# Softmax over 32768 columns: each block of eight partitions takes every sixteenth 64 KB half row, in place of one half row per partition in order

## The chip, the cores and the metric

The kernel runs on one core of one Trainium2 chip. The metric is the device time of one execution in microseconds (us), lower is better. Verdicts use the fast runs alone, with a 95% interval. Ratios are the mean time of one kernel's fast runs over that of the kernel before in the same rounds, so they are not quite the ratios of the medians quoted beside them.

## The reference, cut to what matters

```python
batch, seq, vocab = 16, 256, 32768          # float32, temperature 1.0
scaled = logits / temperature
scaled = scaled - scaled.max(axis=-1, keepdims=True)
exp_scaled = np.exp(scaled)
return exp_scaled / exp_scaled.sum(axis=-1, keepdims=True)
```

There are 4096 rows of 128 KB. All of the input (536.87 MB) has to come in, and as much has to go out.

## The kernel before

A row is cut into two halves of 64 KB, and 128 half rows make a group, one on each partition. A group is loaded in two chunks of 128 x 8192 elements (4 MB, 32 KB on each partition). Six chunk buffers keep loads and stores running side by side. Maximum and sum are exchanged between the two partitions of a row with a shuffle.

```python
_SPLIT = 2
_CW = 8192
_BUFS = 6
_LAST_DMA = 4096
# ...
    x = xf.rearrange("n (h v) -> (n h) v", h=_SPLIT)
    o = of.rearrange("n (h v) -> (n h) v", h=_SPLIT)
# ...
    def load(i: int) -> None:
        g, c = divmod(i, C)
        xs = xpool.tile([P, CW], fp32, tag="x", name="xs")
        slots[i] = xs
        for s, n in spans(CW, _LAST_DMA if g in (0, G - 1) else CW):
            tc.keep_in_program_order(
                nc.sync.dma_start(
                    out=xs[:, s : s + n],
                    in_=x[g * P : (g + 1) * P, c * CW + s : c * CW + s + n],
                )
            )
# ... store(i) is the mirror image; only the last group is stored in 2 MB pieces
    def combine(v, op) -> None:
        for j in range(n_rounds):                    # one round
            mask = [i ^ (1 << j) for i in range(32)]
            nc.vector.stream_shuffle(out=v[:, j + 1 : j + 2], in_=v[:, j : j + 1], mask=mask)
# ...
    order = [("L", i) for i in range(min(_BUFS, n_chunks))] + [("S", 0)]
    for i in range(1, n_chunks):
        order.append(("S", i))
        if i + _BUFS - 1 < n_chunks:
            order.append(("L", i + _BUFS - 1))
```

So six chunks of loads are issued before any store. From then on one store and one load follow each other on one queue.

Of the kernel before, what the change touches and what calls it, by code (L numbers as in the profile page):

```python
# [6 lines left out]


_SPLIT = 2
_CW = 8192  # L10
_BUFS = 6
_PIECE = 8192
# [5 lines left out]
def kernel(  # L18
# [8 lines left out]
    P = nc.NUM_PARTITIONS  # L27
# [6 lines left out]
    xf = logits.flatten_outer_dims()  # L34
    of = out.flatten_outer_dims()
    N, V = xf.shape
    W = V // _SPLIT
    CW = min(_CW, W)
    C = W // CW
    assert W * _SPLIT == V and CW * C == W and (N * _SPLIT) % P == 0  # L40
    x = xf.rearrange("n (h v) -> (n h) v", h=_SPLIT)
    o = of.rearrange("n (h v) -> (n h) v", h=_SPLIT)
    G = N * _SPLIT // P
    n_chunks = G * C
    n_rounds = _SPLIT.bit_length() - 1
# [6 lines left out]
    def spans(total: int, step: int) -> list[tuple[int, int]]:  # L52
        return [(s, min(step, total - s)) for s in range(0, total, step)]
# [4 lines left out]
# [5 lines that stand above are left out]
            tc.keep_in_program_order(  # L63
                nc.sync.dma_start(  # L64
                    out=xs[:, s : s + n],
                    in_=x[g * P : (g + 1) * P, c * CW + s : c * CW + s + n],
                )
            )

    def store(i: int) -> None:  # L70
        g, c = divmod(i, C)
        xs = slots.pop(i)
        for s, n in spans(CW, _LAST_DMA if g == G - 1 else CW):
            tc.keep_in_program_order(
                nc.sync.dma_start(  # L75
                    out=o[g * P : (g + 1) * P, c * CW + s : c * CW + s + n],
                    in_=xs[:, s : s + n],
                )
            )

    def combine(v, op) -> None:
        for j in range(n_rounds):
            mask = [i ^ (1 << j) for i in range(32)]
            nc.vector.stream_shuffle(  # L84
                out=v[:, j + 1 : j + 2], in_=v[:, j : j + 1], mask=mask
            )
            nc.vector.tensor_tensor(  # L87
                out=v[:, j + 1 : j + 2],
                in0=v[:, j : j + 1],
                in1=v[:, j + 1 : j + 2],  # L90
                op=op,
            )
# [30 lines left out]
    def factors(g: int) -> None:  # L123
        nm, ssum, ee, f, ttj = stats[g]
        nMh = spool.tile([P, 1 + n_rounds], fp32, tag="nMh", name="nMh")
        Sh = spool.tile([P, 1 + n_rounds], fp32, tag="Sh", name="Sh")
        rS = spool.tile([P, 1], fp32, tag="rS", name="rS")
        with tc.high_priority():
            nc.vector.tensor_reduce(out=nMh[:, 0:1], in_=nm, axis=X, op=A.min)  # L129
            combine(nMh, A.min)  # L130
            nc.scalar.activation(  # L131
                out=ee,
                in_=nm,
                func=Exp,
                bias=nMh[:, n_rounds : n_rounds + 1],
                scale=-1.0,
            )
            nc.vector.tensor_tensor_reduce(  # L138
                out=ttj,
                in0=ee,  # L140
                in1=ssum,
                scale=1.0,
                scalar=0.0,
                op0=A.mult,
                op1=A.add,
                accum_out=Sh[:, 0:1],
            )
            combine(Sh, A.add)
            nc.vector.reciprocal(out=rS, in_=Sh[:, n_rounds : n_rounds + 1])  # L149
            nc.vector.tensor_scalar_mul(out=f, in0=ee, scalar1=rS)  # L150
# [28 lines left out]
    for kind, i in order:  # L179
        if kind == "L":  # L180
            load(i)
            loaded = i + 1
        else:
            g = i // C
            if g > done:
                while nxt < (g + 1) * C:
                    assert nxt < loaded
                    exps(nxt)
                    nxt += 1
                factors(g)  # L190
                done = g
            scales(i)
            store(i)
# [35 lines left out]
```

## Time and profile before

| | before |
|---|---|
| median of 4 runs | 2494.8 us (2492.84 to 2495.53) |
| DMA, share of 16 engines' span | 99.9% |
| DVE, ACT busy | 60%, 56% |
| bytes moved | 1073.74 MB |
| 32 KB packets (32000 of them) | median 1213 ns, mean 1215 ns |

The next lines are from the page of the kernel before. They are the engines' busy times; the rate of the DMA in 40 equal slices of the span; its queue (packets, MB, share of 16 engines' time); and the chain of work that ended last, as shares of the span.

```profile
DVE 1487.4 (60%) x964; ACT 1405.0 (56%) x455; POOL 0.2 (0%) x4
...
GB/s 412 433 430 432 429 431 432 433 433 434 433 434 432 435 432 435 432 435 431 436 431 435 432 434 433 434 433 433 433 433 433 433 433 434 434 433 434 432 431 368
...
q1 hardware_dynamic: 37728, 1073.76, 99.9%
...
DMA 96%; SPq 1%; ACT 1%; DVE 1%; issue 1%; ACTq 0%
```

The chain is nearly all DMA, and the rate is flat at about 433 GB/s from the second slice to the last but one. The compute engines have 40% to spare, so they do not matter here. The packet records say why the rate is flat: almost every 32 KB packet took the same 1213 ns, which is 27.0 GB/s for an engine and 432 GB/s for sixteen.

The first loads, in the timeline of the kernel before (start, duration, engine, line, operation; the reduction is the first work on loaded data):

```profile
0.73 3.92 SPq L64 DMA_DIRECT2D xs<-in_logits_dram  x8
...
12.89 8.69 DVE L107 TENSOR_REDUCE nm<-xs 128x1 f32<-128x8192 f32 x1 [12.89 <-DMA xs<-in_logits_dram]
```

What the DMA-issuing queue waited for, in us in total, times, and the longest:

```profile
SPq L64 <- DMA out_dram<-xs: 2246.9, 122, 19.6
```

### The profile page before, as it was taken

The numbers are of one execution on the slowest core, as the hardware profiler recorded it, in microseconds if no ns is written. First come the engines' busy times: TensorE is split into PE (matmuls) and PEld (weight loads), VectorE is DVE, ScalarE is ACT, GpSimd is POOL, SyncE is SP. The second block draws the span as 40 slices with busy tenths as digits, with TensorE's granted clock in tenths as the row PEclk, the third lists the DMA queues.
The fourth block names the chain that finished last, engine by engine and source line by source line (L and its number), as shares of the span: only waits on it lengthen the run. The fifth ranks groups of instructions, "written<-read, shape, count | busy, mean of one in ns | idle before, by whom it ended". The sixth has DMA issues, their size and how long they took to land.

```text
span 2493.8 us, 2234 instructions
## 1 busy us (share of the span) xinstructions
DVE 1487.4 (60%) x964; ACT 1405.0 (56%) x455; POOL 0.2 (0%) x4
## 2 busy tenths in 40 slices
DVE  7655565556655566555665566655666566655663
ACT  5665554655556555565555655555546555465553
POOL 0000000000000000000000000000000000000000
DMA  9999999999999999999999999999999999999998
GB/s 412 433 430 432 429 431 432 433 433 434 433 434 432 435 432 435 432 435 431 436 431 435 432 434 433 434 433 433 433 433 433 433 433 434 434 433 434 432 431 368
DMA packets 37745, 1073.90 MB, mean 431 GB/s; under 512 B 4192, under 2 KB 4192, under 8 KB 4192
## 3 DMA queue, kind: packets, MB, share of 16 engines
q1 hardware_dynamic: 37728, 1073.76, 99.9%
q14 instruction: 17, 0.14, 0.0%
HBM read 536.87 MB, written 536.87 MB: 431 GB/s over the span
## 4 chain that ended last, share of the span: by engine, by line
DMA 96%; SPq 1%; ACT 1%; DVE 1%; issue 1%; ACTq 0%
DMA out_dram<-xs 93%; DMA xs<-in_logits_dram 2%; SPq L64 1%; DVE nm L107 1%; ACT xs L163 1%; ACT xs L114 0%; ACTq L224 0%; SPq L75 0%; DVE f L150 0%; ACT ee L131 0%; DVE rS L149 0%; DVE Sh L87 0%; DVE ttj L138 0%; DVE Sh L84 0%; DVE Sh L138 0%
## 5 line engine op out<-in xcount | busy, mean ns | idle before, releaser
L114 ACT ACTIVATE xs<-xs,nm 128x8192 f32<-128x8192 f32 (+1 forms) x130 | 912.1, 7016 | 972.4 <-DVE nm L107 972.4
L107 DVE TENSOR_REDUCE nm<-xs 128x1 f32<-128x8192 f32 (+1 forms) x130 | 1111.6, 8551 | 527.3 <-DMA xs<-in_logits_dram 527.3
L163 ACT ACTIVATE xs<-xs,f 128x4096 f32<-128x4096 f32 (+1 forms) x130 | 468.1, 3648 | 71.4 <-DVE f L150 71.4
L160 DVE TENSOR_SCALAR xs<-xs,f 128x4096 f32<-128x4096 f32 (+1 forms) x130 | 295.7, 2318 | 3.7 <-DVE f L150 1.8
L138 DVE CUSTOM_DVE_ANT_0 ttj<-ee,ssum 128x2 f32<-128x2 f32 x64 | 10.3, 161 | 423.8 <-ACT ee L131 423.8
L114 ACT ACTIVATION_READ_ACCUMULATOR xs<-xs,nm 128x1 f32 x130 | 24.2, 186 | 0.0
L131 ACT ACTIVATE ee<-nm,nMh 128x2 f32<-128x2 f32 x64 | 17.9, 280 | 0.0
L150 DVE TENSOR_SCALAR f<-ee,rS 128x2 f32<-128x2 f32 x64 | 14.6, 229 | 2.2
L149 DVE RECIPROCAL rS<-Sh 128x1 f32<-128x1 f32 x64 | 10.5, 164 | 2.2
L87 DVE TENSOR_TENSOR nMh<-nMh 128x1 f32<-128x1 f32 x64 | 10.2, 160 | 2.2
L87 DVE TENSOR_TENSOR Sh<-Sh 128x1 f32<-128x1 f32 x64 | 10.2, 160 | 2.2
L129 DVE TENSOR_REDUCE nMh<-nm 128x1 f32<-128x2 f32 x64 | 9.9, 155 | 2.2
L84 DVE STREAM_SHUFFLE nMh<-nMh 128x1 f32<-128x1 f32 x64 | 9.7, 151 | 0.0
L84 DVE STREAM_SHUFFLE Sh<-Sh 128x1 f32<-128x1 f32 x64 | 9.7, 151 | 0.0
L114 ACT ACT_TABLE_LOAD x1 | 1.3, 1283 | 12.9 <-DMA xs<-in_logits_dram 12.9
L138 DVE DVE_READ_ACCUMULATOR2_ANT Sh<- 128x1 f32 x64 | 5.3, 84 | 0.0
L84 DVE LOAD_MASK_SELECT Sh<-Sh x64 | 0.9, 14 | 2.8
L84 DVE LOAD_MASK_SELECT nMh<-nMh x64 | 0.9, 14 | 2.7
L210 POOL MEMSET const-bfloat16-1.0<- 128x1 bf16 x1 | 0.1, 102 | 0.0
L210 POOL MEMSET const-uint8-127<- 128x1 uint8 x1 | 0.1, 102 | 0.0
L210 POOL MEMSET const-float32-0.0<- 128x1 f32 x1 | 0.1, 99 | 0.2 <-issue 0.2
L210 POOL MEMSET const-float32-1.0<- 128x1 f32 x1 | 0.1, 99 | 0.0
## 6 DMA issues: line engine op xcount, KB each, us to landing
out_dram<-xs SPq DMA_DIRECT2D x126, 4096.0 KB, 38.2
xs<-in_logits_dram SPq DMA_DIRECT2D x124, 4096.0 KB, 29.0
xs<-in_logits_dram SPq DMA_DIRECT2D x8, 2048.0 KB, 22.3
out_dram<-xs SPq DMA_DIRECT2D x4, 2048.0 KB, 26.7
```

The source lines that it names most:

```text
L64: nc.sync.dma_start(out=xs[:, s : s + n], in_=x[g * P : (g + 1) * P, c * CW + s : c * CW + s + n],)
L84: nc.vector.stream_shuffle(out=v[:, j + 1 : j + 2], in_=v[:, j : j + 1], mask=mask)
L87: nc.vector.tensor_tensor(out=v[:, j + 1 : j + 2], in0=v[:, j : j + 1], in1=v[:, j + 1 : j + 2], op=op,)
L107: nc.vector.tensor_reduce(out=nm[:, k : k + 1], in_=xs[:, s : s + n], axis=X, op=A.max, negate=True)
L114: nc.scalar.activation(out=xs[:, s : s + n], in_=xs[:, s : s + n], func=Exp, bias=nm[:, k : k + 1], scale=inv_t, accum_out=ssum[:, k : k + 1],
L129: nc.vector.tensor_reduce(out=nMh[:, 0:1], in_=nm, axis=X, op=A.min)
L131: nc.scalar.activation(out=ee, in_=nm, func=Exp, bias=nMh[:, n_rounds : n_rounds + 1], scale=-1.0,)
L138: nc.vector.tensor_tensor_reduce(out=ttj, in0=ee, in1=ssum, scale=1.0, scalar=0.0, op0=A.mult, op1=A.add, accum_out=Sh[:, 0:1],)
L149: nc.vector.reciprocal(out=rS, in_=Sh[:, n_rounds : n_rounds + 1])
L150: nc.vector.tensor_scalar_mul(out=f, in0=ee, scalar1=rS)
L160: nc.vector.tensor_scalar_mul(out=xs[:, s : s + cut], in0=xs[:, s : s + cut], scalar1=f[:, k : k + 1])
L163: nc.scalar.activation(out=xs[:, s + cut : s + n], in_=xs[:, s + cut : s + n], func=Copy, scale=f[:, k : k + 1],)
```

## The change

The intent is that DMA engines which are neighbours work on half rows which are neighbours in DRAM. Partition 8a+b now holds half row a+16b of its group, so the DRAM side of each DMA has three dimensions, 16 x 8 x columns. The two halves of a row then lie eight partitions apart.

```diff
+_OUTER = 16
+_INNER = 8
 ...
-    x = xf.rearrange("n (h v) -> (n h) v", h=_SPLIT)
-    o = of.rearrange("n (h v) -> (n h) v", h=_SPLIT)
+    x = xf.rearrange(
+        "(g b s) (h v) -> g (s h) b v", h=_SPLIT, b=_INNER, s=_OUTER // _SPLIT
+    )
+    o = of.rearrange(
+        "(g b s) (h v) -> g (s h) b v", h=_SPLIT, b=_INNER, s=_OUTER // _SPLIT
+    )
 ...
-                    in_=x[g * P : (g + 1) * P, c * CW + s : c * CW + s + n],
+                    in_=x[g, :, :, c * CW + s : c * CW + s + n],
 ...
-                    out=o[g * P : (g + 1) * P, c * CW + s : c * CW + s + n],
+                    out=o[g, :, :, c * CW + s : c * CW + s + n],
 ...
-            mask = [i ^ (1 << j) for i in range(32)]
+            mask = [i ^ (_INNER << j) for i in range(32)]
```

More of the change, by code (lines that the diff above doesn't have):

```diff
@@ L39 @@
     C = W // CW
-    assert W * _SPLIT == V and CW * C == W and (N * _SPLIT) % P == 0
-    x = xf.rearrange("n (h v) -> (n h) v", h=_SPLIT)
-    o = of.rearrange("n (h v) -> (n h) v", h=_SPLIT)
+    assert W * _SPLIT == V and CW * C == W and (N * _SPLIT) % P == 0 and _OUTER * _INNER == P
+    x = xf.rearrange(
[4 more added lines that the diff above has]
+    )
     G = N * _SPLIT // P
```

## The prediction

> What bounds the kernel now. The DMA. The page gives DMA busy 99.9% of 16 engines' span, 431 GB/s over 2493.8 us and 432 to 436 in the middle slices; DVE is busy 60%, ACT 56%. The chain of waits is 93% landings of the store, each about 38.25 us for one 4 MiB store and one 4 MiB load, back to back. The trace's packets are 32 KB half-row pieces, nearly all of exactly 1213 ns: 27.0 GB/s for each engine, 432 GB/s for 16. [...]better HBM locality can save only the ramp and the tail: 1073.74 MB at 432 GB/s is 2485 us by this estimate, so at most about 0.5% is to be had.
>
> What the change does. Compute is untouched: same instruction counts, same shapes, same 32 KB packets; the two STREAM_SHUFFLEs of a group cost 151 ns each[...]. DMA issues, now with a three-dimensional DRAM side, may cost more than the 0.49 us each read from the first eight; with 262 issues and an otherwise waiting SP queue that is off the chain.
>
> What it may break is which engine moves which partitions. [...]each should fall to half rate, 2426 ns a packet[...]. In the trace the lags between engines, read from the 16 landings of each DMA, are about 0.4 us at the start and then stay for hundreds of us (eight engines within 0.5 us, the others up to 10 us late at the end), so nothing in the kernel forces pairs apart or together. Full lockstep would make the kernel 2 x 2485 = 4970 us[...]. [...]
>
> Weighing: conflict-free or self-sorting pairs, within 2%, 0.36; conflict through part or all of the run, 0.62; a real gain over 2% contradicts the packet rate, 0.02. Predicted 2850 us, 8 in 10 between 2485 and 4600.
>
> What would show each step. Packets: [...]durations spread between 1213 and about 2430 ns and GB/s falls below 432 from the first loads on; the page's DMA busy share stays near 99%, because packets take longer. DVE and ACT busy times unchanged (1487 and 1405 us). SP waits grow on store landings. If it is wrong: packets stay 1213 ns and every slice about 433 GB/s.
>
> What would make this wrong. [...]HBM may dislike the new order[...], which would also lengthen packets and would need an experiment to tell apart.

The forecast came to 2850 us (2485 to 4600), a weighing between two ends that stand on the trace: about 2495 us if no engine slows another (the time of the kernel before), and 2 x 2485 = 4970 us if every packet took 2426 ns, twice the measured 1213 ns, to the end. That better HBM locality can save only the ramp and the tail is an estimate from the even 1213 ns alone; experiment 1, at 2495.75 us, shows no gain. "Each" is an engine in step with another that slows it; "pairs" are such engines. The shuffles took 151 ns in both kernels, with either mask.

## More of the kernel before

Windows of the kernel before (stretch, length, busy times of DVE, ACT and POOL, clock, DMA share, GB/s). Up to about 50 us there are only loads.

```profile
20.00:60.00 40.00, 38.12 (x22) 33.57 (x10) 0.00 (x0) 1.00 1.02 434
60.00:100.00 40.00, 32.50 (x25) 31.76 (x12) 0.00 (x0) 1.00 0.99 424
...
2000.00:2400.00 400.00, 241.24 (x152) 224.67 (x72) 0.00 (x0) 1.00 1.00 433
```

## The result, and the profile after

The changed kernel takes 2635.95 us in the median of 4 runs (2605.82 to 2641.83), against 2494.8 us. The ratio is 1.0541, interval 1.0473 to 1.0609: slower. Its own runs spread over 36 us, where those of the kernel before spread over 3 us. The profiled run is the fastest of them (span 2604.0 us, 110.2 us more than before).

The same lines from the page of the changed kernel:

```profile
DVE 1487.8 (57%) x964; ACT 1405.2 (54%) x455; POOL 0.2 (0%) x4
...
GB/s 210 230 283 418 406 430 434 434 430 430 433 432 431 433 434 434 433 433 432 434 433 432 433 433 434 434 433 431 433 434 434 433 431 433 434 433 432 431 387 284
...
q1 hardware_dynamic: 37728, 1073.76, 99.8%
...
DMA 91%; DVE 2%; another core or an unknown queue 2%; SPq 2%; ACT 1%; issue 0%; ACTq 0%; DVEq 0%
```

The compute is untouched and the DMA is as "busy" as before. The busy share does not show how fast the packets go: it is 1.00 at 210 GB/s (60 to 100 us) and 1.00 at 432 GB/s (2000 to 2400 us). The rate shows the loss, and it lies at the two ends. Each slice is 65.1 us. The first six slices fall short of 433 GB/s by 621 GB/s in sum, and 621/433 x 65.1 gives 93 us; the last two by 195, which gives 29 us. The same sums for the kernel before (slices of 62.3 us; 31 and 67 GB/s short) are 4 us and 10 us. The difference is 89 us at the start and about 20 us at the end, 109 of the 110 us. In between nothing is lost in this run. It is the fastest one, and no trace of the others was kept; their median is 141 us up, so some 31 us more stand in no trace of this kernel. The trace of experiment 2 (the same split, 2630.67 us) loses, by the same sum, 95 us at the start, 24 us in the middle and 30 us at the end, so a slower run can lose in the middle too.

The first loads in the timeline of the changed kernel, and windows of it:

```profile
0.73 5.19 SPq L71 DMA_DIRECT2D xs<-in_logits_dram  x8
...
23.00 8.69 DVE L114 TENSOR_REDUCE nm<-xs 128x1 f32<-128x8192 f32 x1 [23.00 <-DMA xs<-in_logits_dram]
```

```profile
20.00:60.00 40.00, 17.84 (x6) 15.90 (x6) 0.00 (x0) 1.00 1.01 215
60.00:100.00 40.00, 23.23 (x15) 21.81 (x7) 0.00 (x0) 1.00 1.00 210
100.00:140.00 40.00, 25.09 (x23) 22.73 (x8) 0.00 (x0) 1.00 1.02 253
140.00:180.00 40.00, 11.51 (x3) 6.39 (x2) 0.00 (x0) 1.00 0.98 284
180.00:220.00 40.00, 12.45 (x14) 16.41 (x6) 0.00 (x0) 1.00 1.00 370
220.00:300.00 80.00, 44.08 (x23) 38.16 (x12) 0.00 (x0) 1.00 1.00 406
...
2000.00:2400.00 400.00, 237.78 (x164) 230.54 (x75) 0.00 (x0) 1.00 1.00 432
```

Issuing costs 0.65 us a DMA in place of 0.49 us, which does not matter: experiment 1, with 0.67 us, takes 2495.75 us. The first chunk lands 10 us later. From 60 to 100 us the rate is 210 GB/s, half of what it was, with a DMA share of 1.00. In that stretch the 32 KB packets that start take 2494 ns on average (before: 1219 ns). The rate rises once stores come in between the loads (the first is issued at 82 us, behind the loads still queued), and after about 350 us it is full.

The queue's wait for stores did not grow in total. Only its longest piece did:

```profile
SPq L71 <- DMA out_dram<-xs: 2246.0, 122, 49.4
```

A last reading comes from the landings. The trace has sixteen landings for each DMA (4192 for 262 DMAs), read here as one for each of 16 engines. These are the landings of the first load and of a DMA at 1570 us in the changed kernel, in us after the first of the sixteen:

```
first load:                 0.0 0.1 0.2 0.3 0.4 0.4 0.6 0.6 0.6 0.6 0.6 0.6 0.6 0.7 0.7 0.8
a DMA in mid-run:           0.0 0.8 4.6 5.2 5.2 5.4 5.7 9.3 9.6 9.8 10.0 10.0 10.1 10.1 10.4 15.0
```

At first all engines are in step. Later they stand in clusters about 5 us apart, which is about four packets of 1213 ns (4.85 us). The spread of a DMA's landings then stays at 15.0 to 15.3 us from 500 to 2400 us.

### The profile page after: what moved, and what is told of

Same layout as the page of the kernel before. It is cut to its first block, busy times and chain, and to the rows that moved or that the text cites. A ratio compares the mean times of both kernels' runs of the same rounds, so it can differ in the third digit from the quotient of the medians.

```text
span 2604.0 us, 2234 instructions
## 1 busy us (share of the span) xinstructions
DVE 1487.8 (57%) x964; ACT 1405.2 (54%) x455; POOL 0.2 (0%) x4
## 2 busy tenths in 40 slices
DMA packets 37745, 1073.90 MB, mean 412 GB/s; under 512 B 4192, under 2 KB 4192, under 8 KB 4192
## 4 chain that ended last, share of the span: by engine, by line
DMA 91%; DVE 2%; another core or an unknown queue 2%; SPq 2%; ACT 1%; issue 0%; ACTq 0%; DVEq 0%
DMA out_dram<-xs 88%; DMA xs<-in_logits_dram 3%; DVE nm L114 2%; SPq L71 1%; ACT xs L121 0%; DVE xs L167 0%; ACT xs L170 0%; ACTq L231 0%; SPq L82 0%; DVE f L157 0%; DVE rS L156 0%; DVE Sh L94 0%; DVE Sh L91 0%; DVE nMh L136 0%
## 5 line engine op out<-in xcount | busy, mean ns | idle before, releaser
L157 DVE TENSOR_SCALAR f<-ee,rS 128x2 f32<-128x2 f32 x64 | 14.6, 229 | 2.2
```

The lines of the kernel that those rows point to most:

```text
L157: nc.vector.tensor_scalar_mul(out=f, in0=ee, scalar1=rS)
```

## The experiments

Theory (engines in step). With 16 as the slowest DRAM dimension, engines that work in step slow each other to about half speed (2494 ns a packet at the start of the changed kernel, 1219 ns in the kernel before); with the right distance between them they don't. What such engines share, and which engines they are, I had inferred; no trace shows it. A forecast that has no name is that of this theory, and "partners" or "pairs" are engines that slow each other. The distance of four packets, which the experiments try, came from the inference. The trace of the changed kernel holds about the same distance: clusters about 5 us apart at 433 GB/s, and four packets are 4.85 us. Rivals: the new order of addresses disturbs HBM; or any three-dimensional DRAM side makes the packets slower ("descriptor theory"); or the start is slow for want of a warm-up.

The trace's packet records do not name the engine. The experiments test the consequences.

### 1. Neighbouring half rows, but 32 x 4

```diff
-_OUTER = 16
-_INNER = 8
+_OUTER = 32
+_INNER = 4
```

> The changed kernel with 32 x 4 in place of 16 x 8: partition 4a+b holds half row a+32b, so [...]the DRAM side still has three dimensions; only the slowest DRAM dimension is 32, not 16. [...]2495 us within 0.5%, packets of 1213 ns from the first loads on. HBM theory[...]: the start stays near 210 GB/s and the time at 2600 to 2640 us. Descriptor theory (any three-dimensional DRAM side is slower): also 2600 to 2640 us.

Measured: 2495.75 us (ratio 1.0005, interval 0.999 to 1.002), packets of 1213 ns in the median and 1215 ns in the mean. A window of this run:

```profile
20.00:60.00 40.00, 38.12 (x22) 33.10 (x10) 0.00 (x0) 1.00 1.01 427
```

Neighbouring blocks of partitions still hold neighbouring half rows, and the DRAM side still has three dimensions. Yet nothing is lost. That refutes the descriptor rival, and the HBM rival in the form "neighbouring 64 KB pieces collide". Long steps in DRAM alone are not the cause either: the four rows of a block lie 2 MB apart here, the eight of the change 1 MB.

### 2 and 3. Half rows in order, in 16 blocks of eight or in 32 blocks of four

These two undo the new order. Each block holds neighbouring half rows as before, and every second block goes to the next group; otherwise all 128 half rows would follow at one even step, as in the kernel before. The exchange is over one partition, as before. The first takes 16 blocks of four rows; the second differs by `r=2, a=32` alone.

```diff
-    x = xf.rearrange("n (h v) -> (n h) v", h=_SPLIT)
+    x = xf.rearrange("(q a d r) (h v) -> q d a (r h) v", h=_SPLIT, r=4, d=2, a=16)
 ...
-                    in_=x[g * P : (g + 1) * P, c * CW + s : c * CW + s + n],
+                    in_=x[g // 2, g % 2, :, :, c * CW + s : c * CW + s + n],
```

(The output side is changed in the same way.)

> The kernel before with its half rows in order: each eight neighbouring partitions hold eight neighbouring half rows (exchange over 1 partition as before), but the sixteen such blocks of a group lie 1 MB apart, every second block going to the next group, so that the DRAM side is 16 x 8. [...]as slow as the change, 2600 to 2650 us, start at about 212 GB/s with packets of 2490 ns. HBM theory: [...]the cause is gone and the time is 2495 us within 0.5%.

> Twin of the run with 16 blocks of 8 half rows: 32 blocks of 4 neighbouring half rows, 512 KB apart, DRAM side 32 x 4. [...]2495 us within 0.5%. Descriptor theory (three-dimensional DRAM side): 2600 to 2650 us, as its twin.

Measured: 16 blocks 2627.75 us (ratio 1.0523, interval 1.0493 to 1.0554); 32 blocks 2496.24 us (ratio 1.0008, interval 0.9991 to 1.0024). Windows of the run with 16 blocks:

```profile
20.00:60.00 40.00, 17.84 (x6) 15.89 (x6) 0.00 (x0) 1.00 1.02 215
60.00:100.00 40.00, 23.23 (x15) 21.81 (x7) 0.00 (x0) 1.00 1.00 210
```

and of its twin with 32 blocks:

```profile
20.00:60.00 40.00, 38.10 (x22) 33.19 (x10) 0.00 (x0) 1.00 1.00 428
```

With blocks 1 MB apart the start is as slow as with blocks 64 KB apart (215 and 210 GB/s in both). So the order of addresses is not the cause. What the two slow kernels share, and the two fast ones don't, is the 16 as the slowest dimension. This settles which part of the change costs the time. Whether it does so through engines in step is the question of experiments 5 to 9.

### 4. No small DMAs

```diff
-_LAST_DMA = 4096
+_LAST_DMA = 8192
```

(in the changed kernel)

> The changed kernel with all DMAs of 4 MB (no 2 MB pieces in the first and last group). [...]the 16 KB packets of the last group bring them back into phase, which costs about 20 us at the end; with 32 KB packets throughout, the rate stays near 433 GB/s until about 30 us before the end, and the span is some 10 to 20 us shorter than the 2604 us of the profiled run, less what the coarser first and last pieces cost in ramp (up to 15 us). If the end's loss has another cause, the slow packets at the end stay.

("Them" are the engines, whose landings stand about 5 us apart in mid-run.)

Measured: 2611.86 us (2603.02 to 2628.33; ratio 1.0478, interval 1.0439 to 1.0517). That is lower than the changed kernel's 1.0541, but the intervals overlap, so no gain is shown. Windows at the end of the changed kernel:

```profile
2480.00:2520.00 40.00, 24.51 (x16) 22.77 (x8) 0.00 (x0) 1.00 1.01 373
```

and of this run:

```profile
2480.00:2520.00 40.00, 23.23 (x15) 23.19 (x8) 0.00 (x0) 1.00 1.00 433
2520.00:2560.00 40.00, 23.78 (x21) 22.51 (x10) 0.00 (x0) 1.00 0.99 415
2560.00:2610.00 50.00, 4.94 (x4) 7.31 (x2) 0.00 (x0) 1.00 0.73 206
```

Whole packets hold the full rate about 40 us longer. The 16 KB packets of the last group do get in each other's way: those that start from 2502 to 2510 us take 1182 ns in the median in the changed kernel, against 611 ns at the end of the kernel before. The expectation was half right, though. What was saved is lost again in the last 50 us, at 206 GB/s with a DMA share of 0.73. There the queue has run dry, and the last stores start with many engines in step again: nine packets start within 0.24 us of each other at 2565 us and take 2366 to 2548 ns. The rate had been expected to hold until 30 us before the end; it held until about 80.

### 5, 6 and 7. Setting engines apart at the start

In experiments 5 to 9 the base is the changed kernel with whole DMAs (2611.86 us). Ahead of all loads, one or two extra loads over fewer partitions, meant for fewer engines, are to give some engines four packets more work. What they load is overwritten by the real load of that buffer. In the first form one load covers 48 partitions, written as 12 x 4 rows, and one 16, written as 4 x 4: meant as four packets for twelve engines, and four more for four of these. The landings agree in number: four, eight and four, in three clusters.

```diff
+    for i in range(min(_BUFS, n_chunks)):
+        early[i] = xpool.tile([P, CW], fp32, tag="x", name="xs")   # used by load(i)
+    for i, engines, first in ((5, 12, 32), (5, 4, 0)):
+        rows = xf[: engines * 2 * 4, :CW].rearrange("(a d b) v -> d a b v", d=2, b=4)
+        tc.keep_in_program_order(
+            nc.sync.dma_start(out=early[i][first : first + engines * 4, :], in_=rows[0])
+        )
```

The second form has `((5, 8, 0),)`: one load over 32 partitions, meant to set one half of the engines back as a whole. The third has the first form's two loads twice, for buffers 5 and 4.

> The changed kernel with whole 4 MB DMAs (2611.9 us) and two extra loads before all others[...]. (What they load is overwritten; the result stays right.) [...]the rate is about 430 GB/s from some 20 us on and the 90 us lost at the start are gone; the end still loses some 20 us and the extra work costs up to 10 us: 2520 to 2550 us. If the slow start is anything else[...]: 2610 to 2640 us with the first 100 us at 210 GB/s.

> The same, but with one extra load[...]. [...]no cure, about 210 GB/s until the first stores and 2600 to 2640 us. If any spread of the engines in time helps[...]: 2520 to 2550 us.

> Both extra loads twice[...]. [...]210 GB/s until the first stores (once the extra loads, some 30 us, are through); then [...]the rate may rise at once to about 430 GB/s: 2560 to 2600 us. If only the size of the spread counts: as the run with four packets, or better, 2520 to 2555 us.

Measured: the first form, with four packets, 2561.62 us (ratio 1.0275, interval 1.026 to 1.0291); halves apart 2633.57 us (1.0561, interval 1.0539 to 1.0583); the third form, with eight packets, 2679.71 us (1.0755, interval 1.0704 to 1.0805). One window of each, in this order:

```profile
20.00:60.00 40.00, 16.79 (x2) 8.50 (x3) 0.00 (x0) 1.00 1.00 267
```

```profile
20.00:60.00 40.00, 16.75 (x2) 8.50 (x3) 0.00 (x0) 1.00 1.01 210
```

```profile
20.00:60.00 40.00, 1.45 (x1) 1.28 (x1) 0.00 (x0) 1.00 1.00 211
```

Moving the halves against each other does nothing (210 GB/s), though their landings lie 6 us apart, and neither does the form with eight packets (211). The form with four packets helps (267). So it is not mere spread that helps: it counts which engines are set apart, and how far. But four packets gave 267 GB/s, not the 430 expected. The run with eight also missed its number: the rate did not jump when the first stores came, and the total was 2680 us where 2560 to 2600 had been expected.

The trace of this run also holds something that the theory does not explain. The loads land every 20 us, in clusters at 0, about 11 and 31 us. So the last two clusters are a whole load apart, which was meant to count as no distance, but the first two only 11 us, about half a load, a distance at which the loads of experiment 9 ran at 419 GB/s. Yet each of the 192 packets of 32 KB that start from 30 to 60 us took over 2.2 us: all sixteen engines kept the slow pace.

### 8. The same set-back without touching SBUF

The landings of experiment 5 showed only about 2 us between two of the clusters. So the set-back is copied within DRAM instead, past SBUF (the on-chip memory with the 128 partitions): five packets meant for twelve engines, then four for four of these, into output rows that are stored again later.

```diff
+    for engines, packets in ((12, 5), (4, 4)):
+        n = engines * 2 * packets
+        src = xf[:n, :CW].rearrange("(a d b) v -> d a b v", d=2, b=packets)
+        dst = of[N - 100 - 2 * n : N - 100 - n, :CW].rearrange("(a d b) v -> d a b v", d=2, b=packets)
+        k = 0 if engines == 12 else 1
+        tc.keep_in_program_order(nc.sync.dma_start(out=dst[k], in_=src[k]))
```

> As the run with partners four packets apart, but the work[...] is copied within DRAM (five packets, then four)[...]; the rows it writes are written again later.[...] the first 100 us of loads run at 380 to 433 GB/s in place of 210, and the whole takes 2510 to 2550 us, against 2612 us without the extra work. If the spread does not cure the start: 2610 to 2640 us.

Measured: 2560.29 us (ratio 1.0265, interval 1.0249 to 1.028). Its window:

```profile
20.00:60.00 40.00, 21.45 (x7) 15.90 (x6) 0.00 (x0) 1.00 1.02 307
```

Better than 267, still short of the 380 expected, and the total is 10 us outside the range.

### 9. Other distances

If engines in step are what makes the start slow, the rate of the load-only stretch must come near the full rate at some distance; I expected it to rise and fall again. The edit is the pair of numbers in `((12, 5), (4, 4))`.

> Six packets copied within DRAM[...], then four[...], ahead of the loads. [...]the load-only stretch is faster than the 310 GB/s of five and four, 340 to 430 GB/s. Otherwise the same 310 GB/s or less.

> Six packets, then five. [...]380 to 433 GB/s in the load-only stretch. Otherwise about 310 GB/s or less.

> Seven packets, then six. [...]300 to 400 GB/s, below the best of the three. If the rate grows simply with the spread of the engines, this one is the fastest of the three.

The window of the base (the run of experiment 4), without any copies:

```profile
20.00:60.00 40.00, 17.84 (x6) 15.90 (x6) 0.00 (x0) 1.00 1.00 211
```

The windows of the three runs, in the order of the expectations:

```profile
20.00:60.00 40.00, 30.97 (x16) 20.49 (x7) 0.00 (x0) 1.00 1.00 419
```

```profile
20.00:60.00 40.00, 22.94 (x7) 15.90 (x6) 0.00 (x0) 1.00 1.00 333
```

```profile
20.00:60.00 40.00, 17.84 (x6) 11.51 (x4) 0.00 (x0) 1.00 1.02 301
```

| packets copied first (meant for 12 engines, for 4) | load-only rate, 20 to 60 us | landings of a later load, clusters in us |
|---|---|---|
| none | 211 GB/s | 0 to 1 |
| 5, 4 | 307 | 0, about 4.6, 9.6 |
| 6, 4 | 419 | 0, about 5.0, 10.0 |
| 6, 5 | 333 | 0, about 6.0, 14.6 |
| 7, 6 | 301 | 0, about 9.1, 18.8 |

There is a peak, and it lies where the clusters are 5.0 us apart, the 4.85 us of four packets. The last two are further apart and slower again. (A gap in us is a smaller part of a load where loads are slow. In the last four rows loads land 13.7, 10.0, 12.3 and 14.1 us apart. So the gaps of 9.1 and 9.7 us in the last row are two thirds of a load, not a whole one, and only with six and four are both gaps half a load.) With six and four the loads run at 419 GB/s from the start, twice the 211 GB/s of the same kernel without the copies. The addresses, split and shapes of these loads are the same, and only the phase of the engines differs, so the phase makes the loss. What the engines share is not shown by any run. The second number missed its own expectation (333, not 380 to 433): I had put the best point one packet too far. Why the rate falls so steeply on the near side, from 419 to 307 GB/s for less than half a microsecond in the clusters, stays open.

Why the copies do not make the whole kernel as fast as the one before is partly plain. The best of the three took 2546.8 us in its single run. It still dips to 358 GB/s between 60 and 100 us, where stores come in (the first is issued at 66 us), and it loses the end as experiment 4 does. Besides, four engines are meant to have ten packets more to do (an estimate of 12 us, from 1213 ns a packet).

### 10. Four buffers

```diff
-_BUFS = 6
-_LAST_DMA = 4096
+_BUFS = 4
+_LAST_DMA = 8192
```

in the changed kernel and, as the control, in the kernel before.

> The changed kernel with whole 4 MB DMAs and four buffers in place of six. If partners stay in step as long as there are only loads, and sort themselves out when stores come between, then the stretch at 210 GB/s lasts four chunks (80 us) in place of six (118 us), and the start loses about 20 us less. If sorting takes a fixed time: the rate still comes up at about 170 to 220 us. Total time is less telling, as four buffers may cost elsewhere: 2580 to 2640 us.

> The kernel before with whole DMAs and four buffers, the control of the changed kernel with four buffers (4117 us). There the queue waited for the computation 2462 us[...]. If it is this that four buffers expose, the kernel before keeps packets of 1213 ns with four buffers and takes 2495 to 2800 us. If four buffers alone are too few[...]: 3500 us or more.

Measured: the changed kernel 4116.69 us (ratio 1.6511 to the kernel before with six buffers), the kernel before 2840.7 us (ratio 1.1386). The question asked, how long the slow start lasts, was overrun by a much larger effect. The changed kernel with four buffers, a window and the longest wait of its issuing queue:

```profile
200.00:600.00 400.00, 148.63 (x91) 137.19 (x43) 0.00 (x0) 1.00 0.95 263
```

```profile
SPq L82 <- DVE xs L167: 2461.7, 64, 72.6
```

The kernel before with four buffers:

```profile
200.00:600.00 400.00, 210.70 (x140) 199.31 (x64) 0.00 (x0) 1.00 0.93 381
```

```profile
SPq L75 <- DVE xs L160: 1924.0, 65, 41.6
```

With four buffers both kernels make their stores wait for the computation once a group, some 65 times, and the DMA has little queued meanwhile. The kernel before pays 346 us for that and keeps packets of 1213 ns in the median. In the changed kernel the median packet takes 2041 ns to the very end, and the engines never settle. The control came out 41 us above its expected range, but far from the 3500 us of the rival. Do the pauses let engines start in step again, as I had supposed? In the control's trace all engines are idle together 63 times, and each time the next sixteen packets start within 0.15 us of each other. In the changed kernel that happens only twice (within 0.27 us, and those packets take 2465 ns on average); some thirty more times fewer than nine packets are under way. So the pauses of the control put its engines in step, but that this is what keeps the changed kernel slow is not isolated by any run.

### 11. Half the groups

```diff
+    G = G // 2
     n_chunks = G * C
```

in the changed kernel and in the kernel before; the rows left out are not written, so the results are wrong.

> The changed kernel with only the first 32 of 64 groups (the other rows are not written, so the result is wrong on purpose). If the loss is at the start and the end, it stays whole: 100 to 150 us more than the kernel before with half the groups (some 1250 us). If it is spread over the run: half of it, about 65 us more (ratio 1.054).

> The kernel before with only the first 32 of 64 groups, the control of the halved changed kernel (wrong on purpose): 1250 to 1260 us, as 1242 us are half of 537 MB twice at 432 GB/s and ramp and tail stay.

Measured: the kernel before 1253.03 us; the changed one 1377.15 us in its one run counted as fast. Three more runs, 1404 to 1408 us, are over 1.5% above that and so count as slow; as this is one core at clock 1.0, it is likely the kernel's own spread, but I compare the fast run alone. It is 124 us above its control, for half the bytes, where the whole kernel is 141 us above. If the loss went with the bytes it would be about 68 us. So most of it is paid once, at the start and the end. One fast run is thin, but the slices of the long run say the same.

## Why the prediction was right or wrong

- **What bounds the kernel: right.** The DMA, through packets of 1213 ns; no compute time moved (DVE 1487.4 to 1487.8 us, ACT 1405.0 to 1405.2 us).
- **What the change breaks: right in what it says of the packets.** The split with 16 as the slowest dimension makes engines that are in step slow each other down. 2426 ns were predicted for a packet in step; 2494 ns were measured. The falling rate from the first loads on and the DMA share near 99% came as written. Experiments 1 to 3 show that the 16 is the cause and the addresses are not; experiment 9 shows that it is the engines' phase. What the engines share, and which of them share it, no run shows; that part was my estimate. The run with eight packets fits only in part.
- **How long it lasts: wrong.** The step that failed reads: "so nothing in the kernel forces pairs apart or together". It was read from the kernel before, where lags stay for hundreds of us (the sixteen landings spread over 6.5 us at 614 us and 7.1 us at 924 us). But in the kernel before no engine is seen to slow another (1213 ns almost throughout). In the changed one the engines move apart within about 300 us of the first stores and then stay apart. The rate rises from 210 to 433 GB/s, and the landings fall into clusters about four packets apart. I had let the conflict run "through part or all of the run" and put the centre at 2850 us, 355 us up; the loss measured is 141 us. The mis-sized term is the duration: the fraction of the run in step. In the profiled run (110 us up) the start costs 89 us and the end about 20 us. The stated range of 2485 to 4600 us holds the result only because it holds nearly everything from no loss to the full lockstep. That engines might soon move apart and leave only a slow start stood in the list of what would make the prediction wrong. The slow start came; what moves the engines apart was not isolated.
- **The end: missed.** That small packets (1182 ns in place of 611) and an emptying queue (packets of 2366 to 2548 ns) bring the conflict back, for about 20 us, was not foreseen.
- **Waits: wrong in a detail.** The queue's waits for stores did not grow in total (2246.9 and 2246.0 us); their longest piece did (19.6 to 49.4 us).
- **No gain to be had: right.** 32 x 4, the layout that keeps neighbouring blocks on neighbouring half rows and the good split, gives 2495.75 us, the same as before. The kernel before remains the best.

Open: what drives the engines apart once loads and stores mix (no run isolates it); why the rate falls so steeply when the distance is less than half a microsecond short; why all sixteen engines kept the slow pace in the run with eight packets, where two of the three clusters lay about half a load apart.

## What to carry to other kernels

When the DRAM side of a 128-partition DMA has more than one row dimension, look at the slowest one: here 16 halved the rate while engines were in step (210 GB/s in place of 433), and 32, with either order of addresses, cost nothing (2495.75 and 2496.24 us). A DMA share near 100% did not show this loss (1.00 at 210 GB/s); read the duration of equal packets, the rate in slices and the spread of a DMA's sixteen landings. Test a layout also with few buffers: the same split cost 5% with six and, against its control, 45% with four.
